# A planner that spaces short TensorE products, and a folding visit in two parts, in an RWKV-7 / HGRN2 layer

## The chip, the cores and the metric

The kernel runs on one NeuronCore of one Trainium2 chip. The metric is the device time of one execution in microseconds (us). Three runs of the kernel before took 1049.75, 1050.35 and 1050.82 us; their median is 1050.35 us. A further execution was profiled, and every duration below is from its trace.

## What is computed

One layer of a hybrid encoder over 512 frames of width 2048, in float32. The reference, cut to what matters:

```python
proj = jnp.einsum('btd,dc->btc', h, w_in[l])
rw = _token_shift(proj[..., :RWKV_COLS], shift_mu[l])
hg = proj[..., RWKV_COLS:]
o_rwkv, v_first = _rwkv7_branch(rw, ...)   # 16 heads of 64: S = S*w + (S a) b^T + v k^T ; o = S r
o_hgrn = _hgrn2_branch(hg, ...)            # 8 heads of 128: gated linear recurrence in chunks of 64
y = jnp.einsum('btc,cd->btd', jnp.concatenate([o_rwkv, o_hgrn], axis=-1), w_out[l])
h = _layer_norm(ALPHA * h + y, ln_w[l], ln_b[l])
```

The two projections hold most of the arithmetic. Both recurrences are evaluated in chunks of 64 frames, with many small products.

## The kernel before, in words

**Long products.** Every float32 operand of a projection is split into a rounded part (`wh`, `xh`) and what is left of it (`wl`, `xl`). ScalarE makes the first, VectorE the second. `three` (L452) then issues three products of 128x128 by 512 columns for each slice, all from L457. A unit of the input projection is 48 such products into one PSUM bank of the tag `main`, of which there are four; four more banks have the tag `mix`. There are 57 units of this kind and two wider ones (`i`), and then the output projection.

**Short products.** The recurrences run between the long products, as generators (threads) that yield one operation at a time; their products go through `mm` (L320, issued at L329). `mm` calls a product narrow where its output has under 128 rows or its contraction under 128. These stand in **visits**: stretches of narrow products between two long ones. The visits of one group of four RWKV heads (there are four groups, each with a pair of HGRN heads beside it) are:

- `quarters` in `rwkv_invert` (L834): twice 32 products of 32x32 by 32 columns (`mix<-big`, then `mix<-inv,inv`);
- `folded` (L751): 64 products of 64x64 by 64 columns into two `main` and two `mix` banks (`main<-zz,big` and `mix<-q,big`, by turns), and the 32 of `beside` (`mix<-big`). `beside` runs in the same visit where two `mix` banks are free (`more`), and otherwise after the copies that empty the first four banks;
- `outputs` (L796): 32 products (`mix<-zz,big`);
- `hgrn_heads` (L955): 32 products (`mix<-q,t`), then twice 64 (`mix<-t` and `mix<-t,t`), then 24;
- the scores in `rwkv_prep` (L628): 16 for each pair of heads.

**The order.** The tile framework does not reorder: the program is written out while the kernel is built, and `Plan` (L63) decides at build time which operation is issued next. It keeps a planned clock for each engine. After each long product `pump` (L201) asks the first thread of every queue for its next operation, and `step` (L161) issues it where its inputs are planned to be there in time. `worth` (L186) keeps the number of changes between long and short products low: a visit may wait up to `HOLD` for a second one to join it, and after a narrow visit no other starts for `REST` (1.5 us of planned time). `landed` (L296) is the test ahead of a visit: a `mix` bank is free and all operands are planned to be there. Nothing limits how many narrow products stand together.

**Evacuation.** A finished bank is read by ScalarE and VectorE (`shift`, L589: at the end `t<-main,pr,t` at L361 on VectorE), and only then can a later unit take the bank. A finished pair of RWKV heads goes through `rwkv_finish` (L903), a finished HGRN head through `hgrn_out`, where VectorE reduces (L365), GpSimd takes the power -1/2 (`rs`, L384) and VectorE scales (`t<-mix,rs`, L352) ahead of four transposes (`mix<-cst,t`, L333).

Of the kernel before, what the change touches and what calls it, by code (L numbers as in the profile page):

```python
# [62 lines left out]
class Plan:  # L63
# [10 lines left out]
    REST = 1.5  # L74
    LEAD = -0.35
    SLACK = 0.6
    EARLY = 0.5

    def __init__(self, room):
        self.clock = {"pe": 0.0, "dve": 0.0, "act": 0.0, "pool": 0.0, "sp": 0.0, "dma": 0.0}  # L80
        self.table = None
        self.mode, self.rest = "main", 0.0
        self.queues, self.waiting, self.hurry = [], {}, False
        self.ready, self.busy, self.banks = {}, {}, set()
        self.room = room
        self.slots = {tag: [(0, 0.0)] * n for tag, n in room.items()}
        self.count, self.used = 0, {}
# [38 lines left out]
    def issue(self, op, way=None):  # L126
        end, s, r, e, f = way or self.best(op)
        f()
        if e == "pe":
            self.mode = op.mode  # L130
            if op.mode == "narrow":
                self.rest = end + self.REST
        if op.table and self.table not in op.table:
            self.table = op.table[0]
        self.clock[e] = end
        self.count += 1
        for x in op.reads + op.writes:
            self.used[x] = self.count
        for w in op.writes:
            self.ready[w] = (end, e)  # L140
            self.busy[w] = (end, e)
        for x in op.reads:
            if self.busy.get(x, (0.0, e))[0] <= end:
                self.busy[x] = (end, e)

    def fetched(self, tile, size):

        self.clock["dma"] = max(self.clock["dma"], self.clock["sp"]) + size * 128 / 360e3
        self.ready[tile.tensor.name] = (self.clock["dma"] + 1.8, "dma")
# [3 lines left out]
        return self.queues[-1]  # L153

    def add(self, queue, gen):
        queue.append([gen, None, False])

    def free(self, tag, n=1):
        return len(self.slots[tag]) >= n
# [1 line left out]
    def step(self, th):  # L161

        now = self.clock["pe"]
        gen, item, held = th
        if not held:
            item = next(gen, StopIteration)
            if item is StopIteration:
                th[0] = None
                return True
            th[1:] = item, True  # L170
        if callable(item):
            if not item():
                return False
        else:
            way = self.best(item)
            end, s, r, e, f = way
            if e == "pe":
                if r > now + self.LEAD or not self.worth(item, now):
                    return False
            elif s > now + self.SLACK or r > max(self.clock[e], now) + self.EARLY:  # L180
                return False
            self.issue(item, way)
        th[2] = False
        return True

# [56 lines left out]
def mixer_kernel(ctx, tc, head, x_r, w_all, par, up, ln_wb, consts, hmask, out):  # L242
    nc = tc.nc
    pe, sc_e, dve, pool = nc.tensor, nc.scalar, nc.vector, nc.gpsimd
# [17 lines left out]
    plan = Plan({**BUFS, **PBUFS})  # L262
# [26 lines left out]
    def room(**need):  # L289

        return lambda: all(plan.free(tag, n) for tag, n in need.items())
# [1 line left out]
    def has(S, *names):  # L293
        return lambda: all(n in S for n in names)

    def landed(*tiles):  # L296

        names = [getattr(t, "tensor", t).name for t in tiles]

        def test():  # L300
            now = plan.clock["pe"] + plan.LEAD
            if not plan.free("mix") or min(plan.slots["mix"])[1] + 0.15 > now:
                return False
            return all(n in plan.ready and plan.seen(n, "pe") <= now for n in names)

        return test

    def send(o, i, cost=0.44):
# [319 lines left out]
    def rwkv_prep(S, p):  # L628
# [79 lines left out]
            yield room(big=1)  # L708
            scores[p // 2] = take("big", [P, 2, 32, 64])
        sc = scores[p // 2]  # L710
        yield landed(bk, ar)
        yield room(mix=2, main=3)
        pss = [take(tag) for tag in ("main", "mix") for h in range(2)]
        for c in range(NCH):
# [36 lines left out]
    def folded(SS, sc):  # L751

        yield lambda: all("zz" in S for S in SS)
        zs, bks = ([S[n] for S in SS] for n in ("zz", "bk"))
        yield room(main=2, mix=2)
        yield landed(*zs, *bks, sc)
        pvs = [take("main") for _ in SS]
        pbs = [take("mix") for _ in SS]
        for half, (z, bk, pv, pb) in enumerate(zip(zs, bks, pvs, pbs)):
            for c in range(NCH):  # L760
                i, cs = half * 16 + 2 * c, slice(c * C, c * C + C)
                for h in range(2):
                    yield mm(pv[hc[h], cs], sc[64:128, 0, i + h], z[64:128, c, hc[h]])
                    yield mm(pb[hc[1 - h], cs], sc[0:64, 0, i + 1 - h], bk[0:64, c, hc[1 - h]])
        more = plan.free("mix", 2)
        prs = []

        def beside():
            prs.extend(take("mix") for _ in SS)
            for half, pr_ in enumerate(prs):  # L770
                for c in range(NCH):
                    for h in range(2):
                        i = half * 16 + 2 * c + h
                        yield mm(pr_[hc[h], c * C : c * C + C], sc[0:64, 0, i], sc[0:64, 1, i])

        if more:
            yield from beside()
        for pv, z, pb, bk in zip(pvs, zs, pbs, bks):
            for h in range(2):
                yield copy(bk[0:64, :, hc[h]], chunks(pb[hc[h]]))  # L780
                yield copy(z[0:64, :, hc[h]], chunks(pv[hc[h]]), scale=-1.0)
            drop(pv, pb)
        if not more:
            yield room(mix=2)
            yield landed(sc)
            yield from beside()

        def keep():
            for half, pr_ in enumerate(prs):
                for h in range(2):  # L790
                    yield copy(sc[0:64, 1, half * 16 + h : half * 16 + 16 : 2], chunks(pr_[hc[h]]))
                drop(pr_)

        yield from keep()

    def outputs(SS, sc):  # L796

        yield room(mix=2)
        pss = [take("mix") for _ in SS]
        for half, (S, po) in enumerate(zip(SS, pss)):  # L800
            z = S["zz"]
            yield lambda z=z: by_now(z)
            for c in range(0, NCH, 2):
                for h in range(2):
                    for e in range(2):
                        yield mm(po[hc[e], c // 2 * P + 64 * h : c // 2 * P + 64 * h + 64],
                                 sc[:, 1, half * 16 + 2 * (c + e) + h], z[:, c + e, hc[h]])
        for S, po in zip(SS, pss):
            yield tt(S["o"], S["o"], tiles(po), ALU.add)
            drop(po, S["zz"])  # L810

    def rwkv_invert(SS, sc_all):
# [19 lines left out]
        yt = a_i[32:64]  # L832

        def quarters(prod, *needs):  # L834
            yield landed(*needs)
            pt = take("mix")
            pq = pt.rearrange("p (i f) -> p i f", f=32)
            for j in range(8):
# [116 lines left out]
    def hgrn_heads(SS, h0):  # L955
# [21 lines left out]
                            :, None].to_broadcast([P, 4, 16 // w, w]),  # L977
                        scores.rearrange("p c (b w) -> p c b w", w=w))

        yield landed(*ks, *qqs)  # L980
        ps = take("mix")
        pss = [ps[:, 192 * i : 192 * i + 192] for i in range(2)]
        for pi, k, qq in zip(pss, ks, qqs):
# [9 lines left out]
        for m, w in enumerate((2, 4, 8, 16, 32, 64, 128)):  # L993
# [19 lines left out]
            if w == 16:  # L1013
# [3 lines left out]
                dgs = [tiles(d) for d in dts]  # L1017
                for d in dts:
                    yield memset(d, 0.0)
            yield landed(*qs, *ks, *kept)  # L1020
            ps = take("mix")
            both = ((hw, kept, kept), (w, ks, qs))
            if w < 64:
# [656 lines left out]
```

## Time and profile before

| What | us |
|---|---|
| Median of the three runs | 1050.35 |
| Profiled execution, as timed | 1049.71 |
| Its span, first to last instruction | 1047.9 |
| TensorE busy in the span | 1034.7 (99%) |
| VectorE busy | 754.5 (72%) |
| ScalarE busy | 436.8 (42%) |

The profile names engines PE (TensorE products), PEld (TensorE weight loads), DVE (VectorE), ACT (ScalarE), POOL (GpSimd) and SP (the engine that issues the DMAs). A row of the timeline gives the start, the duration, the engine, the line, the operation with output<-inputs, and how many rows alike were merged (x64); a bracket at its end gives the engine's idle time before it and what ended that. The end of a product is modelled: products overlap, so a cost is taken here from start to start. A product of two plain float32 operands is one row of the program and two records in the trace: the 32 products of `mix<-inv,inv` are x64 there. A long product is one record.

### The profile page before, as it was taken

What the parts mean: (1) busy time and instruction counts of PE and PEld (TensorE: products, weight loads), DVE (VectorE), ACT (ScalarE), POOL (GpSimd) and SP (SyncE); (2) the same over time, 40 slices, a digit from 0 to 9 for tenths busy, and PEclk for the clock granted to TensorE, in tenths of its full rate; (3) what the DMA queues carried; (4) which work ended last, traced back from release to release, by engine and by line L of the source; (5) the groups of instructions that cost most, each with busy time, mean ns of one, the idle gap of its engine ahead of it and who ended that gap; (6) DMA issues with size and microseconds to landing.
All of it is one profiled execution on the core that took longest, in us unless ns stands there. A gap on an engine that the chain in (4) does not pass through costs nothing.

```text
span 1047.9 us, 19640 instructions
## 1 busy us (share of the span) xinstructions
PE 1034.7 (99%) x7708; PEld 857.5 (82%) x7708; DVE 754.5 (72%) x1599; ACT 436.8 (42%) x817; POOL 41.8 (4%) x77
## 2 busy tenths in 40 slices
PE   9999999999999999999999999999999999999997
PEld 7888888888888888878888788888888888888885
DVE  7474898767759988667689767775999886526456
ACT  6444434543443355353533364435335444223321
POOL 0000001001000010010000100100001011000000
PEclk9999999999999999999999999999999999999999
DMA  9135342133253432224443222344342245445613
GB/s 332 53 103 130 90 104 85 60 93 99 77 140 94 123 87 68 87 74 113 112 116 104 82 73 73 105 110 106 105 117 81 64 157 183 145 129 170 193 60 131
DMA packets 98061, 116.03 MB, mean 111 GB/s; under 512 B 67120, under 2 KB 68912, under 8 KB 97840
## 3 DMA queue, kind: packets, MB, share of 16 engines
q1 hardware_dynamic: 97824, 114.57, 37.1%
q8 instruction: 61, 1.00, 0.4%
q14 instruction: 32, 0.26, 0.1%
q10 hardware_dynamic: 144, 0.20, 0.1%
HBM read 99.92 MB, written 7.34 MB: 102 GB/s over the span
## 4 chain that ended last, share of the span: by engine, by line
PE 93%; DMA 2%; DVE 2%; SPq 1%; issue 1%; ACT 0%; POOL 0%; DVEq 0%
PE main L457 70%; PE mix L329 11%; PE mix L457 8%; PE main L1205 3%; DMA wr<-w_all 2%; PE main L329 1%; PE mix L333 1%; SPq L310 1%; DMA q<-head 0%; DVE t L352 0%; DVE wl L352 0%; DVE inv L361 0%; DMA g<-ksq 0%; ACT t L342 0%; DVE q L361 0%
## 5 line engine op out<-in xcount | busy, mean ns | idle before, releaser
L457 PE MATMUL main<-xh,wh 128*128 128x512 f32 x864 | 339.6, 393 | 1.9 <-DVE t L361 1.9
L457 PE MATMUL main<-xh,wl 128*128 128x512 f32 x864 | 341.2, 395 | 0.0
L457 PE MATMUL main<-xl,wh 128*128 128x512 f32 x864 | 339.7, 393 | 0.0
L342 ACT ACTIVATE wh<-wr 128x512 fp32r<-128x512 f32 x299 | 186.5, 627 | 244.7 <-PE main L457 193.6
L352 DVE TENSOR_TENSOR wl<-wr,wh 128x512 fp32r<-128x512 f32 x299 | 203.3, 682 | 75.1 <-ACT wh L342 73.6
L457 PEld LDWEIGHTS main<-xh,wh 128*128 128x128 f32 x864 | 162.4, 188 | 35.3 <-DVE t L361 2.3
L457 PEld LDWEIGHTS main<-xh,wl 128*128 128x128 f32 x864 | 162.4, 188 | 33.3 <-DVE wl L352 0.3
L457 PEld LDWEIGHTS main<-xl,wh 128*128 128x128 f32 x864 | 162.3, 188 | 33.2
L457 PE MATMUL main<-wl,xh 128*128 128x512 f32 (+1 forms) x262 | 102.2, 390 | 0.3 <-DVE wl L352 0.3
L457 PE MATMUL main<-wh,xh 128*128 128x512 f32 (+1 forms) x262 | 102.1, 390 | 0.0
L457 PE MATMUL main<-wh,xl 128*128 128x512 f32 (+1 forms) x262 | 101.8, 388 | 0.0
L457 PEld LDWEIGHTS main<-wl,xh 128*128 128x128 f32 x262 | 49.2, 188 | 10.3 <-DVE wl L352 0.6
L457 PEld LDWEIGHTS main<-wh,xh 128*128 128x128 f32 x262 | 49.2, 188 | 10.2 <-ACT wh L342 0.2
L457 PEld LDWEIGHTS main<-wh,xl 128*128 128x128 f32 x262 | 49.2, 188 | 9.8
L361 DVE SCALAR_TENSOR_TENSOR bd<-mix,pc,bd 64x64 f32<-64x64 f32 x112 | 31.7, 283 | 17.1 <-PE mix L329 15.0
L343 ACT ACTIVATE t<-main,om 128x512 f32<-128x512 f32 x33 | 22.2, 686 | 51.6 <-PE main L457 42.4
L342 ACT ACTIVATE t<-mix 64x128 f32<-64x128 f32 (+2 forms) x65 | 17.6, 272 | 56.6 <-PE mix L329 28.2
L352 DVE TENSOR_TENSOR inv<-inv 64x30 f32<-64x30 f32 (+14 forms) x120 | 38.5, 321 | 2.8
L352 DVE TENSOR_TENSOR inv<-inv,inv 64x30 f32<-64x30 f32 (+14 forms) x120 | 38.5, 321 | 2.7
L361 DVE SCALAR_TENSOR_TENSOR t<-main,pr,t 128x511 f32<-128x511 f32 x33 | 24.3, 745 | 19.7 <-ACT t L343 19.6
L352 DVE TENSOR_TENSOR t<-t,tot 128x256 f32<-128x256 f32 x96 | 37.5, 417 | 0.3
L343 ACT ACTIVATE t<-main 128x512 f32<-128x512 f32 x32 | 18.6, 595 | 32.5 <-PE main L457 32.3
(218 smaller groups left out, 1311.9 us busy)
## 6 DMA issues: line engine op xcount, KB each, us to landing
wr<-w_all SPq DMA_DIRECT2D x156, 512.0 KB, 3.7
q<-head SPq DMA_DIRECT2D x15, 448.0 KB, 6.1
q<-q SPq DMA_DIRECT2D x128, 32.0 KB, 2.7
g<-x_r SPq DMA_DIRECT2D x16, 256.0 KB, 4.0
spill<-g SPq DMA_DIRECT2D x12, 256.0 KB, 3.7
t<-spill SPq DMA_DIRECT2D x12, 256.0 KB, 4.3
out<-q SPq DMA_DIRECT2D x12, 256.0 KB, 2.5
zz<-ksq SPq DMA_DIRECT2D x64, 32.0 KB, 3.0
```

The costliest lines, as they stand in the source:

```text
L310: nc.sync.dma_start(o, i)
L329: return Op([("pe", cost, lambda: pe.matmul(o, l, r, start=start, stop=stop, **kw))], [l, r], [o], mode="narrow" if narrow else "main" if ...
L333: return Op([("pe", 0.11, lambda: pe.transpose(o, i, ident))], [i], [o])
L342: return "act", cost, lambda: sc_e.activation(o, i, f, scale=scale)
L343: return "act", cost, lambda: sc_e.activation(o, i, f, scale=scale, bias=bias)
L352: return dve_op([a, b], o, lambda: dve.tensor_tensor(o, a, b, f), base=0.16 if o.shape[0] < P and size(o) == C and o.tensor.name in tags e ...
L361: return dve_op([a, b], o, lambda: dve.scalar_tensor_tensor(o, a, s, b, f1, f2), per=0.00113, base=0.085 if o.shape[0] == P else 0.25 if s ...
L457: pe.matmul(ps, l, r, start=first and i == 0, stop=last and i == 2)
L1205: pe.matmul(pss[a], *ops, start=k == 0 and low == of == 0, stop=k == KT - 1 and low == 1)
```

## The change

Two things change. The planner gets a bound: `Plan.short` holds the planned ends of the narrow products of late, and `room_for` lets a batch of n begin only where none has ended in the last 3.0 us of planned time, or where those that have and n together are at most 68. Each test ahead of a visit now says how many narrow products follow it (`n=` in `landed`, or `batch`), and `step` asks `room_for` at the first of them. And `folded` no longer runs `beside` in its first visit: the copies come first, and the 32 products of `beside` always wait for two `mix` banks. No operation is added or removed. Lines of the changed kernel are 15 to 17 higher (L457 is L474, L329 is L346, L333 is L350).

```diff
+    BURST, WITHIN = 68, 3.0
...
+        self.short = []
...
             if op.mode == "narrow":
                 self.rest = end + self.REST
+                self.short.append(end)
...
+    def room_for(self, n):
+
+        since = self.clock["pe"] - self.WITHIN
+        while self.short and self.short[0] < since:
+            self.short.pop(0)
+        return not self.short or len(self.short) + n <= self.BURST
...
     def step(self, th):
...
         if callable(item):
             if not item():
                 return False
+            th[3] = getattr(item, "batch", th[3])
         else:
             way = self.best(item)
             end, s, r, e, f = way
             if e == "pe":
+                if th[3] and item.mode == "narrow":
+                    if not self.room_for(th[3]):
+                        return False
...
             self.issue(item, way)
+            if item.mode == "narrow":
+                th[3] = 0
...
-    def landed(*tiles):
+    def landed(*tiles, n=0):
...
+        test.batch = n
         return test
...
-        yield landed(bk, ar)
+        yield landed(bk, ar, n=16)
...
-        yield landed(*zs, *bks, sc)
+        yield landed(*zs, *bks, sc, n=64)
...
-        more = plan.free("mix", 2)
...
-        if more:
-            yield from beside()
         for pv, z, pb, bk in zip(pvs, zs, pbs, bks):
             for h in range(2):
                 yield copy(bk[0:64, :, hc[h]], chunks(pb[hc[h]]))
                 yield copy(z[0:64, :, hc[h]], chunks(pv[hc[h]]), scale=-1.0)
             drop(pv, pb)
-        if not more:
-            yield room(mix=2)
-            yield landed(sc)
-            yield from beside()
+        yield room(mix=2)
+        yield landed(sc, n=32)
+        yield from beside()
...
-            yield landed(*needs)
+            yield landed(*needs, n=32)
...
-        yield landed(*ks, *qqs)
+        yield landed(*ks, *qqs, n=32)
...
-            yield landed(*qs, *ks, *kept)
+            yield landed(*qs, *ks, *kept, n=64 if w < 64 else 24)
```

The orders of TensorE and VectorE are the same up to the second visit of the first group, and then differ nearly everywhere, since each visit that moves changes what the planner finds ready next. Three places follow.

**The first group, TensorE.** Before, the first 32 products of `quarters` (`mix_1648<-big`) and the first 64 of `hgrn_heads` (`mix_1692`) are one visit between long products:

```order
L457 MATMUL main_1273<-wh_1615,xh_82 128x512
L329 MATMUL mix_1648<-big_694 32x32 x32
L329 MATMUL mix_1692<-t_1049 32x16 x16
L329 MATMUL mix_1692<-t_1258 32x16 x16
L329 MATMUL mix_1692<-t_954,t_1050 32x16 x16
L329 MATMUL mix_1692<-t_1161,t_1259 32x16 x16
L457 MATMUL main_1273<-wl_1616,xh_82 128x512
```

In the changed kernel the 32 stand alone, long products follow (here the first three), and the 64 come later:

```order
L346 MATMUL mix_1648<-big_694 32x32 x32
L474 MATMUL main_1273<-wl_1616,xh_82 128x512
L474 MATMUL main_1273<-wh_1615,xl_98 128x512
L474 MATMUL main_1296<-wh_1615,xh_82 128x512
```

```order
L474 MATMUL main_1273<-wh_1632,xh_83 128x512
L346 MATMUL mix_1692<-t_1049 32x16 x16
L346 MATMUL mix_1692<-t_1258 32x16 x16
L346 MATMUL mix_1692<-t_954,t_1050 32x16 x16
L346 MATMUL mix_1692<-t_1161,t_1259 32x16 x16
L474 MATMUL main_1273<-wl_1633,xh_83 128x512
```

Between the two visits there are now 12 long products. The same is done at each place where narrow products stood more than 68 together.

**The folding visit of the second group, TensorE.** Before, the last of its 64 products (`main_3935`, `mix_3937`) are followed at once by the 32 of `beside`:

```order
L329 MATMUL main_3935<-zz_3613,big_2882 64x64
L329 MATMUL mix_3937<-q_3117,big_2882 64x64
L329 MATMUL mix_4017<-big_2882 64x64 x16
L329 MATMUL mix_4018<-big_2882 64x64 x16
L457 MATMUL main_3791<-xh_75,wl_3777 128x512
```

In the changed kernel long products stand ahead of the 32 (11 of them, here the last three):

```order
L474 MATMUL main_3992<-xh_70,wh_3881 128x512
L474 MATMUL main_3992<-xl_86,wh_3881 128x512
L474 MATMUL main_3992<-xh_70,wl_3882 128x512
L346 MATMUL mix_3989<-big_2795 64x64 x16
L346 MATMUL mix_3990<-big_2795 64x64 x16
L474 MATMUL main_3992<-xh_71,wh_3881 128x512
```

Over the whole program the visits of narrow products go from 28 to 33, and the largest from 128 products to 64: one visit more in the first, third and fourth group each, two more in the second.

**The third HGRN head, TensorE.** Its last product (`mix_4825<-t`) and the long products behind it. Before, the unit `main_4752` has 11 products left, and then the unit `main_4866` begins (here from the third-last of the 11):

```order
L457 MATMUL main_4752<-xh_83,wh_4786 128x512
L457 MATMUL main_4752<-xl_99,wh_4786 128x512
L457 MATMUL main_4752<-xh_83,wl_4787 128x512
L457 MATMUL main_4866<-xh_68,wh_4816 128x512
L457 MATMUL main_4866<-xl_84,wh_4816 128x512
L333 MATMUL mix_4865<-cst,t_3389 128x128 x4
```

In the changed kernel the same head's last product (`mix_4807<-t`) is followed by 21 long products of `main_4765`, the head's four transposes and 4 more long products, before the next unit `main_4876` begins:

```order
L474 MATMUL main_4765<-xh_81,wl_4800 128x512
L350 MATMUL mix_4852<-cst,t_3432 128x128 x4
L474 MATMUL main_4765<-xh_82,wl_4800 128x512
L474 MATMUL main_4765<-xh_83,wh_4799 128x512
L474 MATMUL main_4765<-xl_99,wh_4799 128x512
L474 MATMUL main_4765<-xh_83,wl_4800 128x512
L474 MATMUL main_4876<-xh_68,wh_4830 128x512
```

What VectorE does for this head stands in the same sequence in both. Before:

```order
L365 TENSOR_REDUCE rs_4837<-t_3389 128x4
L358 TENSOR_SCALAR rs_4837<-rs_4837 128x4
L352 TENSOR_TENSOR wl_4846<-wr_4703,wh_4845 128x512
L352 TENSOR_TENSOR t_3389<-mix_4825,rs_4837 128x512
L361 SCALAR_TENSOR_TENSOR t_4859<-main_4212,pr,t_4859 128x511
```

and in the changed kernel:

```order
L382 TENSOR_REDUCE rs_4819<-t_3432 128x4
L375 TENSOR_SCALAR rs_4819<-rs_4819 128x4
L369 TENSOR_TENSOR wl_4831<-wr_4757,wh_4830 128x512
L369 TENSOR_TENSOR t_3432<-mix_4807,rs_4819 128x512
L378 SCALAR_TENSOR_TENSOR t_4840<-main_4232,pr,t_4840 128x511
```

The last row of each is the evacuation that frees the bank for `main_4866` and `main_4876`. Counted in long products from the head's end, the bank is wanted after 11 before, and after 25 and four transposes in the changed kernel.

Near the end of the input projection the last group is later: its `outputs` stand at the 3143rd long product before and at the 3181st in the changed kernel, and the transposes of the last HGRN head at the 3269th and the 3280th. The output projection begins at the 3185th, takes 12 long products for each of its 16 slices in its first quarter, and needs the last head's slice as the 15th. The last 60 rows of TensorE are the same in both but for buffer numbers.

More of the change, by code (lines that the diff above doesn't have):

```diff
@@ L155, in add @@
     def add(self, queue, gen):
-        queue.append([gen, None, False])
+        queue.append([gen, None, False, 0])
     def free(self, tag, n=1):
@@ L163, in step @@
         now = self.clock["pe"]
-        gen, item, held = th
+        gen, item, held = th[:3]
         if not held:
@@ L169, in step @@
                 return True
-            th[1:] = item, True
+            th[1:3] = item, True
         if callable(item):
@@ L801, in outputs @@
             z = S["zz"]
-            yield lambda z=z: by_now(z)
+            test = lambda z=z: by_now(z)
+            test.batch = 32 - 16 * half
+            yield test
             for c in range(0, NCH, 2):
```

## The prediction

> **What bounds the kernel now.** I read the page first, then TensorE's list of waits, then the timeline around the waits that have no releaser.
>
> ```profile
> span 1047.9 us, 19640 instructions
> PE 1034.7 (99%) x7708; PEld 857.5 (82%) x7708; DVE 754.5 (72%) x1599; ACT 436.8 (42%) x817; POOL 41.8 (4%) x77
> q8 instruction: 61, 1.00, 0.4%
> PE 93%; DMA 2%; DVE 2%; SPq 1%; issue 1%; ACT 0%; POOL 0%; DVEq 0%
> ```
>
> TensorE is busy 99% of the span and 93% of the chain that ended last. Its products are the same in the changed kernel, so only three things can move the time: idle time of TensorE, the price of going between long and short products, and stretches that run slower than they must. The idle time is small, and the waits view says where it is (cause, total, times, longest):
>
> ```profile
> PE main L457 <- DVE t L361: 1.9, 1, 1.9
> ...
> PE mix L329 <- issue: 1.3, 3, 0.8
> PE main L329 <- issue: 1.3, 1, 1.3
> ...
> PE mix L329 <- DMA g<-ksq: 0.6, 1, 0.6
> ```
>
> Four waits, 2.6 us, are "issue": TensorE waited for nothing that the profile shows, and all four are at L329, the short products. The timeline shows them inside the largest visits (start, duration, line, x records):
>
> ```profile
> 182.23 0.39 PE L457 MATMUL main<-xl,wh 128*128 128x512 f32 x1
> 182.55 0.70 PE L329 MATMUL mix<-t 128*32 128x16 f32 x62
> ...
> 187.67 0.27 PE L329 MATMUL main<-zz,big 64*64 64x64 f32 x1 [1.28 <-issue]
> ...
> 188.29 0.50 PE L457 MATMUL main<-xh,wl 128*128 128x512 f32 x1
> 188.63 0.39 PE L457 MATMUL main<-xh,wh 128*128 128x512 f32 x1
> ...
> 386.83 0.27 PE L329 MATMUL main<-zz,big 64*64 64x64 f32 x1
> 391.86 0.50 PE L329 MATMUL mix<-big 64*64 64x64 f32 x9 [0.77 <-issue]
> 392.29 0.50 PE L457 MATMUL main<-xh,wl 128*128 128x512 f32 x1
> ...
> 591.51 0.75 PE L329 MATMUL mix<-inv,inv 32*32 32x32 f32 x64
> 592.92 0.54 PE L329 MATMUL mix<-t 128*32 128x16 f32 x43 [0.37 <-issue]
> 594.00 0.50 PE L457 MATMUL main<-wh,xh 128*128 128x512 f32 x1
> ...
> 600.14 0.71 PE L329 MATMUL mix<-t 128*32 128x16 f32 x62
> 601.58 0.25 PE L329 MATMUL mix<-t,t 128*32 128x16 f32 x6 [0.22 <-issue]
> 601.75 0.50 PE L457 MATMUL main<-wh,xl 128*128 128x512 f32 x1
> ```
>
> What runs dry is told by two rows. One queue brought instructions in 61 packets; TensorE's 7708 products and 7708 weight loads by 61 are 253 for a packet. And the two pauses of the third group stand a whole number of such packets apart:
>
> ```profile
> 592.91:601.57 8.66, 8.44 (x256) 6.97 (x255) 5.10 (x18) 3.51 (x9) 0.00 (x0) 1.00 0.22 64
> ```
>
> 256 products and 255 loads (one is recorded just outside) lie between them, twice 256 instructions. So I read a pause as TensorE at the end of what was brought, waiting for the next 256 instructions. A short product of the program is two products and two loads, so 64 of them use up one packet, and 128 in one visit two.
>
> [...]
>
> **The change, part by part: the pauses that go.** Visits that did not pause give the clean price, from the first short product to the next long one:
>
> ```profile
> 179.11 0.78 PE L329 MATMUL mix<-inv,inv 32*32 32x32 f32 x64
> 179.81 0.50 PE L457 MATMUL main<-wh,xh 128*128 128x512 f32 x1
> ...
> 191.01 2.08 PE L329 MATMUL mix<-big 64*64 64x64 f32 x64
> 193.03 0.50 PE L457 MATMUL main<-xl,wh 128*128 128x512 f32 x1
> ...
> 410.59 0.71 PE L329 MATMUL mix<-t 128*32 128x16 f32 x62
> ...
> 411.79 0.50 PE L457 MATMUL main<-xl,wh 128*128 128x512 f32 x1
> ...
> 800.87 0.27 PE L329 MATMUL main<-zz,big 64*64 64x64 f32 x1
> ...
> 805.23 0.50 PE L457 MATMUL main<-xl,wh 128*128 128x512 f32 x1
> ```
>
> 32 of `inv` 0.70, 64 of `t` 1.20, `beside` alone 2.02, folding with `beside` 4.36, so folding alone 2.34 us. Against these:
>
> - first group, `t` and folding: 188.29 - 182.55 = 5.74, clean 1.20 + 2.34 = 3.54, lost 2.20;
> - second group, folding with `beside`: 392.29 - 386.83 = 5.46, lost 1.10;
> - third group: 594.00 - 591.51 = 2.49 against 0.70 + 1.20, lost 0.59; 601.75 - 600.14 = 1.61 against 1.20, lost 0.41.
>
> Together 4.3 us. The lower bound is the idle time alone, 2.6; where two kinds meet in a visit the seam may cost a little, so I take 4.2. In the changed kernel no visit has more than 64 short products, or one packet. That is no safety by itself: the visit of 600.14 had 64 and paused 0.41, its predecessor having ended at 594.00. I leave one such pause in: +0.4 (0 to 0.8).
>
> **The visits that are added.** 33 instead of 28. A visit takes 0.32 us from the last long product's start to the first short one's (182.23 to 182.55) where a long product follows another after 0.23, and the first long product behind it takes 0.34 (188.29 to 188.63): 0.09 + 0.11 = 0.20 us, five times +1.0. It can't be below nothing, since each is a change there and back; it would be 5 x 0.32 = 1.6 if the whole step into a visit were lost.
>
> **Copies before `beside`.** No operation is added. The eight copies that empty the four banks start some 2 us earlier, the four copies of `beside` some 2.5 us later (11 long products in the order shown). What waits for them is the scan and `outputs`, and TensorE has long products meanwhile: 0. If that cover fails, it is the end of the last group, below.
>
> **The wait at 457.68.** The largest wait is at a place that the change rearranges:
>
> ```profile
> 455.13 0.39 PE L329 MATMUL mix<-t,t 128*128 128x128 f32 x2
> ...
> 457.68 0.39 PE L457 MATMUL main<-xh,wl 128*128 128x512 f32 x1
> 459.98 0.50 PE L457 MATMUL main<-xh,wh 128*128 128x512 f32 x1 [1.92 <-DVE t L361]
> ...
> 457.16 1.39 POOL L384 TENSOR_TENSOR rs<-rs,mhalf 128x4 f32<-128x4 f32 x1 [3.81 <-DVE rs L358]
> ...
> 458.58 0.69 DVE L352 TENSOR_TENSOR t<-mix,rs 128x512 f32<-128x512 f32 x1 [0.90 <-POOL rs L384]
> 459.19 0.74 DVE L361 SCALAR_TENSOR_TENSOR t<-main,pr,t 128x511 f32<-128x511 f32 x1
> ```
>
> The evacuation of a bank stood on VectorE behind `t<-mix,rs`, which waited for GpSimd; so the bank came free 459.98 - 455.5 = 4.5 us after the head's last product (455.13 + 0.39). TensorE wanted it after 11 long products, 2.5 us. The order of the changed kernel keeps VectorE's sequence (the five rows shown) and puts 25 long products and four transposes there: 25 x 0.23 + 0.4 = 6.1 us, over 4.5. This wait goes: 2.30 - 0.23 = 2.07, and 0.11 for the slow start after it, -2.2.
>
> **New waits.** A rearranged order will miss somewhere else. The waits for data in the middle of the program were 1.9 and 0.6, 2.5 us in all. I can't place the next ones from the order, so I take 1.0, with bounds 0 and 2.8.
>
> **The sum.** -4.2 + 0.4 + 1.0 - 2.2 + 1.0 = -4.0 us. The profiled execution took 1049.71 (span 1047.9 and 1.8 around it), so it would be 1045.7; the median of the runs is 0.64 higher, 1050.35, and becomes **1046.4**. About 0.2% (2.1 us) is what can be told from no change: faster is below 1048.25, slower above 1052.45. Bounds of these terms: -4.3 + 0 + 1.0 - 2.2 + 0 = -5.5, 1044.9; and -2.6 + 0.8 + 1.0 - 2.2 + 2.8 = -0.2, 1050.1.
>
> **The rivals.**
>
> *Another wait of the same size comes back.* The mechanism of 457.68 (evacuation behind a GpSimd power) stands at each of eight HGRN heads. Then -4.2 + 0.4 + 1.0 + 1.0 = -1.8: 1048.5, on the edge. For: the planner cannot see the lag. Against: it happened once in eight.
>
> *The pauses are not bound to the length of a visit.* If a pause comes at some refills whatever stands there, all four stay: +1.0 - 2.2 + 1.0 = -0.2, 1050.1. For: the visit of 600.14 was within the bound and paused. Against: the two longest pauses are in visits of 128 and 96, and `inv`, `t` and `beside` alone ran clean. [...]
>
> *Slower: each visit that holds a refill pauses.* 64 short products hold a refill almost always, and the changed kernel has 15 visits of 56 or 64 where there were 7 of 64 and 6 above. If each of the 15 lost what 600.14 or 591.51 lost, 0.41 to 0.59, that is 6.2 to 8.9 us: -4.2 + 1.0 + 7.5 - 2.2 + 1.0 = +3.1, 1053.5. It decides from (4.2 - 1.0 + 2.2 - 1.0) / 0.5 = 9 pausing visits on. Against: of the rows above, 410.59 held 64 and ran clean.
>
> *The last group is late.* Its `outputs` come 38 long products, 8.6 us, later. VectorE and TensorE around there (stretch; length, busy us of PE, PEld, DVE):
>
> ```profile
> 845.00:881.00 36.00, 36.00 (x205) 30.35 (x201) 28.05 (x55) 16.05 (x31) 7.41 (x4) 1.00 0.45 150
> 881.00:906.00 25.00, 25.00 (x114) 20.76 (x113) 13.38 (x22) 9.39 (x17) 0.00 (x0) 1.00 0.61 225
> ```
>
> VectorE has 8.0 and 11.6 us spare, TensorE has no idle time, and the last head's transposes move by only 11 products, to 73 (16.6 us) ahead of the product that needs them. If VectorE lost all 8.6 us there, TensorE would wait up to that: +4.6, 1055. It decides only past the spare.
>
> **How the numbers follow.** Forecast 0.68, a wait of the same size back 0.15, pauses stay 0.10, every refill pauses 0.04, last group late 0.03. The range from 1044.8 to 1049.8 takes in the forecast's bounds but for the case that all are worst at once, and a wait of the same size back; it leaves out the last three. Faster: 0.68 and half of 0.15, less some of the edge, 0.74; slower 0.06 (0.04 and 0.03, some of which end near the bound); same 0.20.
>
> **What would show it.** In the profile after: no "issue" row above 0.5 us among TensorE's waits, at most 1.3 us together; folding alone at 2.3 to 2.4 us and `beside` at 2.0 from first short product to next long one; no wait for L378 (the old L361) near the third head. It would be wrong if pauses over 0.5 us stand in visits of 64, or if data waits of TensorE grow past 3 us.

## The result, and the profile after

The changed kernel took 1043.14 us (median of four runs, 1043.11 to 1044.48) where the kernel before took 1050.59 beside it: a ratio of 0.9932, 95% interval 0.9915 to 0.9949. Its profiled execution took 1043.15. The prediction was 1046.4 with a range down to 1044.8: the direction is right, the gain is larger than its range allows.

Timed again later, it took 1043.07 us (five runs, 1042.71 to 1043.30) beside 1049.1: 0.9940, interval 0.9926 to 0.9954. The gain is then 6.0 us rather than 7.45, since the kernel before is the one that varies (1048.27 to 1050.28 there).

The page of the changed kernel, its span, busy times, instruction queue and chain:

```profile
span 1041.4 us, 19628 instructions
PE 1033.5 (99%) x7708; PEld 856.9 (82%) x7708; DVE 756.2 (73%) x1595; ACT 435.9 (42%) x821; POOL 40.3 (4%) x77
q8 instruction: 61, 1.00, 0.4%
PE 98%; DVE 1%; DMA 0%; SPq 0%; ACT 0%; issue 0%; DVEq 0%
```

TensorE's busy time moved by 1.2 us (1034.7 before), the span by 6.5: idle time went. The whole list of TensorE's waits is now two rows (cause, total, times, longest), neither of which is an "issue" or lies in the recurrence:

```profile
PE mix L346 <- ACT ksq L1437: 1.5, 1, 1.5
PE mix L1170 <- DVE inv L1168: 1.1, 1, 1.1
```

The timeline of the first group shows what became of the visit of 182.55, which held `t` and the folding and paused 1.28 us:

```profile
186.06 0.39 PE L474 MATMUL main<-xh,wl 128*128 128x512 f32 x1
186.38 0.70 PE L346 MATMUL mix<-t 128*32 128x16 f32 x62
...
187.58 0.50 PE L474 MATMUL main<-xh,wh 128*128 128x512 f32 x1
...
191.35 0.39 PE L474 MATMUL main<-xl,wh 128*128 128x512 f32 x1
191.67 0.27 PE L346 MATMUL main<-zz,big 64*64 64x64 f32 x1
...
194.30 0.50 PE L474 MATMUL main<-xh,wl 128*128 128x512 f32 x1
```

`t` alone takes 1.20 us from its first short product to the next long one, the folding alone 2.63, with 17 long products between: 3.83 in place of 5.74. The other three foldings take 2.52, 2.40 and 2.56 us.

### The profile page after: what moved, and what is told of

The parts are those of the page before. It is cut to its first block, busy times and chain, and to the rows that moved or that the text cites. A ratio compares the mean times of both kernels' runs of the same rounds, so it can differ in the third digit from the quotient of the medians.

```text
span 1041.4 us, 19628 instructions
## 1 busy us (share of the span) xinstructions
PE 1033.5 (99%) x7708; PEld 856.9 (82%) x7708; DVE 756.2 (73%) x1595; ACT 435.9 (42%) x821; POOL 40.3 (4%) x77
## 4 chain that ended last, share of the span: by engine, by line
PE 98%; DVE 1%; DMA 0%; SPq 0%; ACT 0%; issue 0%; DVEq 0%
PE main L474 75%; PE mix L346 11%; PE mix L474 8%; PE main L1220 3%; PE main L346 1%; PE mix L350 1%; DMA q<-head 0%; DVE inv L378 0%; SPq L327 0%; DVE inv L369 0%; ACT xh L359 0%; DVE stats L1577 0%; DVEq L1691 0%; DVE mv L1385 0%; DVE mv L374 0%
## 5 line engine op out<-in xcount | busy, mean ns | idle before, releaser
L474 PE MATMUL main<-xh,wh 128*128 128x512 f32 x864 | 340.9, 395 | 0.0
L474 PE MATMUL main<-xh,wl 128*128 128x512 f32 x864 | 340.0, 394 | 0.0
L474 PE MATMUL main<-xl,wh 128*128 128x512 f32 x864 | 339.7, 393 | 0.0
L474 PEld LDWEIGHTS main<-xh,wl 128*128 128x128 f32 x864 | 162.4, 188 | 33.2
L474 PEld LDWEIGHTS main<-xh,wh 128*128 128x128 f32 x864 | 162.4, 188 | 33.1
L474 PEld LDWEIGHTS main<-xl,wh 128*128 128x128 f32 x864 | 162.4, 188 | 33.0
L474 PE MATMUL main<-wl,xh 128*128 128x512 f32 (+1 forms) x262 | 102.4, 391 | 0.0
L474 PE MATMUL main<-wh,xl 128*128 128x512 f32 (+1 forms) x262 | 101.9, 389 | 0.0
L474 PE MATMUL main<-wh,xh 128*128 128x512 f32 (+1 forms) x262 | 101.7, 388 | 0.0
L474 PEld LDWEIGHTS main<-wh,xh 128*128 128x128 f32 x262 | 49.2, 188 | 10.0
L474 PEld LDWEIGHTS main<-wl,xh 128*128 128x128 f32 x262 | 49.2, 188 | 9.8
L474 PEld LDWEIGHTS main<-wh,xl 128*128 128x128 f32 x262 | 49.2, 188 | 9.8
```

What stands on the lines that cost most here:

```text
L474: pe.matmul(ps, l, r, start=first and i == 0, stop=last and i == 2)
```

## The experiments

Three theories were tested. **Supply:** a pause is TensorE at the end of a packet of 256 instructions, and comes where it uses them faster than the next arrive. **Seam:** a pause belongs to a visit's length, or to where two kinds of short product meet. **Order:** apart from the pauses, the gain is in data waits that a new order happens not to have.

### Each half of the change alone

The bound off, the folding split kept:

```
-    BURST, WITHIN = 68, 3.0
+    BURST, WITHIN = 10 ** 9, 3.0
```

> The changed kernel with the folding split kept and the bound on short products off (68 becomes a number never reached). By the planner's order four visits hold more than 64 short products again: three of 96 and one of 128. Theory (supply: a visit that uses up 256 instructions faster than the next 256 come pauses): the visit of 128 and at least two of the three of 96 pause, 1 to 2 us and 0.4 to 1.1 us lost, 2 to 4 us together; less 4 visits fewer at 0.2 us: 1044.3 to 1046.3 us. Rival (pauses belonged to the old folding visit, where `beside` stood in it): no pause, 1042.3 us. For the data waits: if their absence in the changed kernel is luck of its order, this order shows some of its own, 0.5 to 3 us; if the change takes them away by itself, none.

Measured: 1049.67 us beside 1049.1, ratio 1.0004 (0.9995 to 1.0013): all of the gain is lost, and the time is above the 1044.3 to 1046.3 that the supply theory gave. TensorE's waits in the middle of the program:

```profile
PE main L474 <- DVE t L378: 1.9, 1, 1.9
...
PE mix L346 <- issue: 1.1, 2, 0.9
...
PE main L346 <- issue: 0.5, 1, 0.5
```

Three pauses are back, 1.6 us idle: in the visit of 128, in one of the three of 96, and in one of 64 (0.24 us at 601.42). The other two visits of 96 lose nothing and 0.2 us, so length alone doesn't make a pause. The old wait at the third head is back too, and behind it the timeline shows something that the first profile didn't:

```profile
458.57 0.76 PE L474 MATMUL main<-xh,wh 128*128 128x512 f32 x1 [1.92 <-DVE t L378]
...
460.83 0.63 PE L474 MATMUL main<-xh,wh 128*128 128x512 f32 x1
461.26 0.63 PE L474 MATMUL main<-xl,wh 128*128 128x512 f32 x1
...
462.32 0.40 PE L474 MATMUL main<-xl,wh 128*128 128x512 f32 x1
```

Long products follow each other after 0.43 us here, not 0.23, and the windows view has a granted clock of 0.50 from 458.60 to 461.90. That costs over 1 us on top of the wait. The head's last product has 11 long products behind it here, as in the kernel before.

The bound kept, `beside` back in the folding visit:

```
+        more = plan.free("mix", 2)
+        if more:
+            yield from beside()
...
-        yield room(mix=2)
-        yield landed(sc, n=32)
-        yield from beside()
+        if not more:
+            yield room(mix=2)
+            yield landed(sc, n=32)
+            yield from beside()
```

> The changed kernel with the bound kept and the folding visit whole as in the kernel before. Three visits of folding with `beside` hold 96 short products, the others at most 64. Theory (supply): each of the three can pause as the one at 386.83 did in the kernel before, 1.1 us lost; two to three of them do: 1043.1 + 2.2 to 3.3 = 1045.3 to 1046.4 us. Rival (the fold was harmless, only `t` next to another kind paused): none pauses, 1043 us. Data waits: 0 to 2 us if their absence is luck of the order.

Measured: 1045.13 us, ratio 0.9960 (0.9948 to 0.9973), 2.0 us above the 1043.1 of the changed kernel, which was timed separately. All three visits of 96 pause, and one data wait is there:

```profile
PE mix L346 <- issue: 1.2, 3, 0.6
...
PE mix L350 <- DVE t L369: 0.4, 1, 0.4
```

So about two thirds of the gain come without the split (0.9960 against 0.9940); the split is worth the three pauses and, in this order, a wait of 0.4.

### The same bound, other orders

```
-    BURST, WITHIN = 68, 3.0
+    BURST, WITHIN = 68, 5.0
```

> The changed kernel with 5 us in place of 3 us for the stretch in which short products are counted: 35 visits, none above 64 short products. Pauses: none above 0.2 us. Two visits more, +0.4 us. What it tells is the data waits of TensorE in another order with the same bound: if their absence in the changed kernel is luck, 0.5 to 3 us of them come back (1043.5 to 1046.5 us); if shorter visits keep the evacuations on time, none (1043.5 us).

and the same with 1.5:

> The changed kernel with 1.5 us in place of 3 us: 35 visits, none above 64 short products, but two visits may stand closer together, so that a packet may come late for the second: 0 to 0.6 us of pauses. Data waits as for 5 us: 0.5 to 3 us if their absence is luck of the order, none otherwise. 1043.5 to 1046.5 or 1043.5 us.

Neither keeps the gain, and both are above every time that was expected: 1050.95 us, 1.0016 (1.0007 to 1.0026), and 1053.27, 1.0040 (1.0027 to 1.0053). With 5 us there is no pause at all, as foreseen, and yet it is 8 us slower than the changed kernel. Its waits in the middle of the program, and the window behind the larger one (PE, PEld, DVE, ACT, POOL busy, granted clock, DMA share, GB/s):

```profile
PE mix L350 <- DVE t L369: 3.5, 1, 3.5
...
PE mix L346 <- DVE bd L378: 0.9, 1, 0.9
```

```profile
458.00:464.50 6.50, 5.69 (x16) 4.67 (x17) 5.28 (x8) 2.91 (x5) 0.00 (x0) 0.50 0.10 40
```

The 3.5 us stand at the third head again. Its transposes (`mix<-cst,t`) follow its last product at once and wait for the `t` that VectorE makes behind the power on GpSimd, as the timeline of the two engines shows:

```profile
456.93 1.01 POOL L401 TENSOR_TENSOR rs<-rs,mhalf 128x4 f32<-128x4 f32 x1 [2.87 <-DVE rs L375]
```

```profile
457.97 0.69 DVE L369 TENSOR_TENSOR t<-mix,rs 128x512 f32<-128x512 f32 x1 [1.12 <-POOL rs L401]
```

Then 6.5 us run at half the clock. Half of that, 3.2 us, as an estimate of what it costs, and the 4.4 us of waits make 7.6 of the 8 us. With 1.5 us the same wait is 2.2 us, and pauses are there too:

```profile
PE mix L350 <- DVE t L369: 2.2, 1, 2.2
...
PE mix L346 <- issue: 1.0, 2, 0.7
PE main L346 <- issue: 0.8, 1, 0.8
```

All its waits and pauses beyond the changed kernel's add up to 5.6 us, and 3.4 us at half the clock behind the third head cost an estimated 1.7; the rest of its 10 us is open.

This is the order theory: neither the bound nor the split takes data waits away. Of five orders with some of the change in them, two (the changed kernel and the bound alone) put enough long products behind the third head, and three did not.

### Moving the packet boundaries

The kernel before with 16 tiny products more at its start, which touch nothing that is used later:

```
+    for _ in range(16):
+        pe.matmul(warm[:32, :32], zero[:32, :32], zero[:32, :32])
```

> The kernel before with 16 tiny 32x32 products (64 instructions) ahead of the first long product, and the same order of everything else. Theory (supply in packets of 256 instructions): every boundary moves 64 instructions, that is 32 product records or 16 short products, earlier. The pause at 592.92, behind 84 records of its visit, comes behind 52, inside `inv`; the one at 601.58, behind 122, comes behind 90; the one at 391.86, behind 183, comes behind 151. Sizes may change, their sum stays within 1.5 us of 2.6; time within 1.5 us of before. Rival (pauses belong to the seam between two kinds of short product, or to the end of a visit): all four stay where they are, to a record.

Measured: 1057.47 us (1054.88 to 1060.41) beside 1049.32, ratio 1.0089 (1.0064 to 1.0114). The same order with 64 instructions ahead is 8 us slower; its profiled execution, at 1054.88, shows 5.2 us of that against the first one before. The pauses:

```profile
PE mix L329 <- issue: 5.0, 4, 1.9
```

One of the three forecast pauses came where it was forecast, behind 151 records at 391.86. The other two did not come at 52 and 90; the third group pauses instead one packet later, behind 180, and two visits that ran clean in the first profile pause now (413.23 and 810.38; the second of them also pauses in two later executions of the kernel before, one packet earlier). So the boundaries moved as the theory says, and no seam held a pause in place; but which boundary pauses, and for how long, was not foreseen. The timeline of the third group:

```profile
593.09 0.75 PE L329 MATMUL mix<-inv,inv 32*32 32x32 f32 x64
593.77 0.72 PE L329 MATMUL mix<-t 128*32 128x16 f32 x63
...
594.33 0.66 PE L329 MATMUL mix<-t,t 128*32 128x16 f32 x51
596.92 0.30 PE L329 MATMUL mix<-t,t 128*32 128x16 f32 x12 [1.93 <-issue]
...
598.67 0.63 PE L457 MATMUL main<-wh,xl 128*128 128x512 f32 x1
...
601.60 0.39 PE L457 MATMUL main<-wh,xh 128*128 128x512 f32 x1
```

A pause of 1.93 us and, 1.3 us later, a stretch of long products at 0.43 us each. The windows view gives it a granted clock of 0.50 from 598.20 to 601.40, and the same from 188.50 to 191.70 behind the first group's pause. The one shown holds eight such products, 0.2 us more each: 1.6 us beside the 1.93.

The changed kernel with 16, 32 and 48 tiny products, its boundaries a quarter, a half and three quarters of a packet away:

> The changed kernel with 16 tiny products (64 instructions) ahead, a quarter of a packet. If the changed kernel is lucky in where its packet boundaries fall, one visit pauses by 0.5 to 1.5 us, as with 32 tiny products (0.84 us in the folding visit of the first group): 1044 to 1045 us. If that one was the exception, none: 1043.3 us.

> The changed kernel with 32 tiny products (128 instructions) ahead, so that packet boundaries fall half a packet away. If no visit of 64 pauses because 64 short products never outrun the supply, no pause above 0.2 us appears and the time stays at 1043.1 (+0.3 for the products themselves). If the changed kernel was lucky in where its boundaries fall, one to four visits pause 0.2 to 0.6 us: 1043.5 to 1045.

> The changed kernel with 48 tiny products (192 instructions) ahead, three quarters of a packet. The same two cases: one pause of 0.5 to 1.5 us (1044 to 1045.3 us), or none (1043.4 us).

Measured: 1044.12, 1045.27 and 1049.43 us. That is not the pauses alone. The added products cost more than I had allowed at the start, where they are slow and hold up the first long ones; their rows in the second and third kernel, and a window of the third at half the clock:

```profile
5.19 2.40 PE L1172 MATMUL mix<-inv 32*32 32x32 f32 x64
```

```profile
4.94 3.22 PE L1172 MATMUL mix<-inv 32*32 32x32 f32 x96
```

```profile
8.00:11.40 3.40, 3.40 (x14) 2.68 (x11) 3.33 (x6) 3.14 (x7) 0.00 (x0) 0.50 1.04 414
```

In the profiles the first visit of `scores` starts 0.7, 2.1 and 4.3 us later than in the changed kernel; what the third loses beyond its profiled 1047.61 in most of its other runs (to 1050.31) I can't place. Behind the start they differ by their pauses: none with 16, and with 32 and 48 one each:

```profile
PE mix L346 <- issue: 0.8, 1, 0.8
```

```profile
PE mix L346 <- issue: 0.3, 1, 0.3
```

Both are in visits of 64 short products (the folding at 193.80, `t` at 182.43). The bound doesn't make a visit safe; the changed kernel's own boundaries fall well.

### More short products of one kind

The second `inv` product of each group issued twice and four times (the repeats write the same values):

```
-                    yield mm(pq[32 * g : 32 * g + 32, j], *prod(8 * g + j))
+                    op = mm(pq[32 * g : 32 * g + 32, j], *prod(8 * g + j))
+                    e, cost, f = op.ways[0]
+                    op.ways = [(e, cost, lambda f=f: [f() for _ in range(times)])]
+                    yield op
```

> The changed kernel with each product of the second `inv` stage of each group issued twice in a row (the second writes the same value again). The visit has 64 short products in place of 32. Clean price 64 product records more at 8.7 ns: 0.56 us a group, +2.2 us in all: 1045.4 us. Theory (supply): 256 instructions in about 1.3 us is within what one packet ahead covers: no pause or up to 0.4 us in one or two groups. Rival (only mixed kinds pause): none.

> The same with each product issued four times: 128 short products of one kind in one visit, 512 instructions, with no seam between kinds. Clean +6.8 us in all: 1049.9 us. Theory (supply): each group's visit pauses once or twice, 1 to 3 us lost a group, 4 to 12 us together beyond the clean price: 1054 to 1062 us. Rival (pauses come at a seam between kinds, not from the count): none, 1049.9 us.

Measured: 1046.82 us without a pause for twice, 1074.33 for four times (one execution each), with a pause in each of the four groups. My clean price was wrong, and with it both times: the repeats cost more than the products they repeat. Four times, the first group's visit:

```profile
182.44 0.39 PE L474 MATMUL main<-xh,wl 128*128 128x512 f32 x1
182.76 3.35 PE L346 MATMUL mix<-inv,inv 32*32 32x32 f32 x162
186.75 3.12 PE L346 MATMUL mix<-inv,inv 32*32 32x32 f32 x94 [0.64 <-issue]
```

```profile
186.00:192.60 6.60, 5.96 (x107) 5.20 (x101) 0.47 (x1) 2.13 (x5) 0.00 (x0) 0.50 0.01 2
```

162 records take 3.16 us from start to start, 19.5 ns each where a plain `inv` takes 8.7; the 94 behind the pause run at half the clock. The time is no test of the theories. The pause is: one kind, no seam, and it stops in the middle. That is against the seam theory.

### Where the pauses stand

In all profiles, those below too, 33 gaps of over 0.3 us inside visits or right behind one (at 196.80 with 1.5 us) are neither waits for data nor steps into a visit. Counting TensorE's records (products, weight loads and its semaphore instructions) in order of their start from the beginning of the trace, the number of the first record behind each gap, and its remainder by 256 (the same all through a row):

```
kernel                 first record behind the gap            remainder
before                 2754, 5826, 8898, 9410                 194
before, second         2754, 5826, 9410, 12482                194
before, third          2754, 5826, 9410, 12482                194
before, 16 tiny        2754, 5826, 6594, 9154, 12738          194
split alone            2754, 6082, 9410                       194
bound alone            3010, 9922, 12482                      194
1.5 us                 2498, 3010, 6338, 12482                194
32 tiny / 48 tiny      3010 / 2242                            194
inv four times         2498, 5826, 10178, 13762               194
```

All 33 stand at the same place in a packet. The traces also hold the packets themselves, as transfers of 16 KiB on the instruction queue: 61 for 15609 records before, 63 for 16112 with `inv` twice, 67 for 17136 with `inv` four times, one for each 256. At each of the 33 gaps the packet due there, counted in order, begins to move 2.2 to 3.2 us, and has landed 1.2 to 1.6 us, before the first record behind the gap; at none of the other 875 such places does TensorE go on sooner than 1.2 us after the landing. So TensorE waits there for that packet, which is the supply theory.

### The kernel before, twice more, and the changed kernel again

> The kernel before, a second profiled execution. Theory (the pauses and the 1.9 us wait vary and at times halve the granted clock of TensorE for some 3.3 us, which makes the scatter of this kernel's runs): pauses in the same four visits at the same records, but of other sizes (sum 1.5 to 5 us in place of 2.6), and where one of them leaves TensorE idle for over 1 us a stretch of about 3.3 us at a granted clock of 0.5 behind it in some executions, 1 to 1.7 us each. Rival (the scatter comes from the transfers at the start and end, which the changed kernel shares): the same pauses within 0.2 us, and no stretch at 0.5.

> The kernel before, a third profiled execution: as for the second. Theory: time and sum of pauses and halved stretches move together from execution to execution. Rival: they don't.

Measured: 1048.84 and 1049.34 us. The second and the third execution of the kernel before, their waits in the middle of the program:

```profile
PE main L457 <- DVE t L361: 1.9, 1, 1.9
...
PE mix L329 <- issue: 1.4, 3, 0.6
...
PE main L329 <- issue: 1.0, 1, 1.0
```

```profile
PE main L457 <- DVE t L361: 1.9, 1, 1.9
...
PE mix L329 <- issue: 1.1, 3, 0.5
...
PE main L329 <- issue: 1.0, 1, 1.0
```

Three pauses are at the same records, of other sizes; that of 592.92 is gone from both and one at 802 is there instead. The two small waits of the first execution, for `g<-ksq` (0.6) and `wl` (0.3), are in neither: they belonged to the execution. The wait at the third head is 1.92 us in all three, and what follows it differs. The 3.3 us behind it, in the second and in the third execution:

```profile
459.28:462.58 3.30, 3.30 (x16) 2.75 (x17) 2.56 (x4) 3.03 (x6) 0.00 (x0) 1.00 0.18 73
```

```profile
458.58:461.88 3.30, 3.30 (x10) 2.71 (x11) 1.99 (x3) 3.00 (x5) 0.00 (x0) 0.52 0.13 51
```

Sixteen products or ten, by the granted clock alone. Behind the same wait, 1.92 us long each time, the granted clock was 1.00 in two executions and 0.52 over these 3.3 us in the third. Time and sum of pauses do not fall in one line over three executions, though (idle 2.6, 2.4 and 2.1 us at 1049.71, 1048.84 and 1049.34), so this explains a part of the scatter, not all of it.

> The changed kernel again, timed beside the kernel before in five rounds. Profiles of three executions of the kernel before differ: the 0.6 us for `g<-ksq` and the 0.3 us for `wl` of the first stand in neither of the other two. Theory A (those two waits and part of the 0.64 us between its profiled execution and its median belong to the execution, not to the order): the gain is below 7.45 us, 5 to 6.5 us, since the wait at 457.68 (2.2), the pauses (4.2) less 1.0 for five visits remain: the changed kernel at 1043 to 1043.6 us beside 1048.6 to 1049.3. Theory B (the order removes them): the gain is 7 to 8 us again, 1041.5 us beside 1049. And its profile shows no pause, or one that was not there in the first execution.

Measured: 1043.07 us, 6.0 below 1049.1; the profile's two waits are those of the first execution, and no pause. That is theory A, and its lower figure.

## Why the prediction was right in direction and short in size

The sum against the profiled executions, span 1047.9 to 1041.4, 6.5 us. "Visits" is the sum, over all visits of a trace, of the time from the start of the last long product ahead to the start of the first behind, less the 0.23 that one long product takes.

| term | forecast | measured | how |
|---|---|---|---|
| pauses -4.2, residual +0.4, five visits +1.0 | -2.8 | -3.0 | visits 72.2 to 68.7, and +0.11 for the slow long product behind each of five |
| wait at 457.68 | -2.2 | -2.2 | row gone, 2.08 and 0.11 |
| new waits | +1.0 | 0 | no row in the list after |
| the two small waits of before | none | -1.1 | start to start 0.6 and 0.5; only in this execution |
| sum | -4.0 | -6.3 | of 6.5 |
| median above the profiled execution | +0.64 | 0.0 | 1043.14 against 1043.15 |

**The pauses that go: right.** The visits sum to 72.2, 72.3 and 71.9 us in the three executions before, and to 68.7 and 68.5 in the two after. The reading of the packets, argued before from two pauses, is shown by the 33 and by the transfers behind them.

**One residual pause of 0.4: fair, and the changed kernel drew none. The price of folding alone, 2.34: too low.** The four foldings took 2.62, 2.52, 2.40 and 2.56 us, 0.7 us more together (0.5 in the second execution), so the sign "folding alone at 2.3 to 2.4 us" held in one of four. That the first row of the table comes so near is in part luck: a pause that did not come made up for a price that was too low. Over four positions of the boundaries the idle time is 0, 0, 0.8 and 0.3 us.

**Five added visits at 0.20, copies before `beside` at nothing: fit.** No wait for the scan or `outputs` appeared; the parts were not measured apart.

**The wait at 457.68: right**, for the reason given. The orders that put too little behind the head have it: 1.9 us with the split alone, 2.2 and 3.5 with the other bounds.

**New waits: this is the step that failed.** "A rearranged order will miss somewhere else" was sized at +1.0 by the waits for data in the middle of the program before, 1.9 and 0.6. There were none. The 0.6 was no measure of what an order costs: it and the 0.3 stood in one execution of three. I left them in the sum as if the changed kernel would keep them, and added another 1.0. As an expectation over orders the term was rather low: the waits that the orders tried here have are 0, 0.4, 1.9, 3.0 and 4.4 us. But it is a draw, and its lower bound was 0 where it could go below: waits of the old order can go as well as come, and 1.1 us went. That the order is a draw is a reading of these five orders; nothing here tells ahead of a run what an order will draw.

**The median's 0.64: also wrong.** It was carried over as if it belonged to the measurement. It belonged to what the change removes, at least in part: pauses of varying size, and a wait of 1.92 us behind which the clock was halved in one execution of three. In the later timing the changed kernel's five runs span 0.6 us and the eight of the kernel before 2.0; in the first, with four runs of each, it was 1.4 and 1.8, so how much of the 0.64 went with the change is not settled.

**The rivals.** A wait of the same size coming back, at 0.15, did not happen here and happened in three of the five orders; its chance was too low. That the pauses stay whatever stands there is wrong: with the changed kernel's boundaries, and with 16 tiny products, none is left. That each refill pauses is wrong: 33 of the 908 such places do so by over 0.3 us. The late last group did not show.

## What to carry to other kernels

Where a profile shows idle time with no releaser inside a run of short instructions, count records to the next such place: if the distances are whole packets (256 records here), shorten the run or spread it, and try a few positions of the boundaries, since 64 harmless instructions at the start were worth 8 us. Judge a scheduling rule by several orders that it gives, not by one, and take the kernel before through more than one profile before its small waits enter a sum. A wait costs its own length, 1.92 us at the third head, and in one of three executions of the kernel before there was a half clock behind it, ten products in 3.3 us where the other two had sixteen.

## What the runs showed of the hardware

**When a packet comes too late.** I took for every boundary, in the fifteen profiles that now exist, the time without the pause in which TensorE went through 40 instructions of one packet and the whole next one, up to the place in the table. Under 3.4 us it paused in 15 of 15 cases, by 0.3 to 2.1 us; between 3.4 and 4.3 in 11 cases and not in 43; above 4.3 in 7 of some 840, by 0.4 to 1.1 us. The 15 ended 3.3 to 4.5 us after the 40 instructions began. In none of the fifteen traces does a packet begin to move more than 298 records ahead of its place, which is why 40 and 256 are counted. In the 15 it began to move 0.9 to 2.0 us into that stretch, in the seven 2.8 to 5.4. So the seven had a transfer that began late, and why it did is open.

**The clock halves behind some waits of 1.9 us and not behind others.** At the end of the waits of 1.92, 2.2 and 3.5 us at the third head (split alone, 1.5 us, 5 us), and behind the pause of 1.93 us with 16 tiny products, TensorE's granted clock was 0.50 for a while and came back by itself. And the same wait of 1.92 us did it in one of three executions of the kernel before. The clock records of the traces say more: the halved stretches inside the program last 3.41 us (seven of them) or 6.83 (four), and in every execution all changes of the clock stand whole multiples of 3.413 us apart (133 of them ahead of the stretch at 458.7 in the third execution, 171 behind it; 305 and 303 from the first clock record to the turn to 0.50 at the end, in the first execution before and in the changed kernel). That steps of this length also run on where the clock doesn't change is my estimate from these distances. Counted on so, one step holds the whole 1.92 us in the third execution, and 1.2 and 1.5 us of it at most in the first and the second, which would explain why one wait does it and its like does not. With 16 tiny products ahead, though, 1.91 us lie within one step too and the clock stayed full, so what is enough is open.

Behind runs of 32x32 products it halved with no idle time just before, in two kernels. With 48 tiny products at the start the clock was at 0.50 for 3.4 us with no pause, and with `inv` four times it halved in the last group while TensorE was busy without a break, 0.8 us before that visit's pause began:

```profile
820.10:824.30 4.20, 4.20 (x243) 4.13 (x244) 2.29 (x7) 0.03 (x1) 0.76 (x2) 1.00 0.38 131
...
824.40:831.10 6.70, 5.52 (x90) 4.74 (x84) 2.07 (x6) 2.35 (x5) 0.00 (x0) 0.50 0.01 2
```

In the first group, too, the clock record turns to 0.50 at 186.03, ahead of the idle time from 186.11 on. So it was not the pause. That it was the products there is a reading of these two runs, and which property of them would count was not tried.
